# Expert choice of a block kernel: one-hot rows written by tensor_scalar, index lookup by comparing candidate rows

## Chip, cores and metric

The kernel runs on one core of a Trainium2 chip. The metric is the device time of one execution in microseconds (us), lower is better. PE is TensorE, PEld its weight loads, DVE is VectorE, ACT is ScalarE, POOL is GpSimd, SP is SyncE.

## The reference, cut to what matters

Two blocks run one after the other on 256 tokens of width 1024. The change touches the feed-forward part of the first block, a product-key expert retrieval over 16384 experts. For each block of 128 tokens:

```python
q = (t @ w_query).reshape(PEER_BLOCK, PEER_HEADS, 2, PEER_DQ // 2)   # 8 heads, two halves of 128
s1 = einsum('thd,nd->thn', q[:, :, 0], k1)                           # 128 scores per half
s2 = einsum('thd,nd->thn', q[:, :, 1], k2)
v1, i1 = lax.top_k(s1, 16)
v2, i2 = lax.top_k(s2, 16)
cand_s = v1[..., :, None] + v2[..., None, :]                         # 16 x 16 sums
cand_i = i1[..., :, None] * 128 + i2[..., None, :]
top_s, pos = lax.top_k(cand_s.reshape(...), 16)
idx = take_along_axis(cand_i.reshape(...), pos)                      # the 16 experts of a head
g = softmax(top_s)
act = gelu(einsum('thkd,td->thk', expert_u[idx], t))
y = einsum('thk,thkd->td', g * act, expert_v[idx])
```

## The kernel before

No expert row is gathered. The kernel computes gelu(u t) for all 16384 experts, 128 experts at a time (a "key row", 128 of them), multiplies by a dense weight W[token, i1, i2] that is zero where an expert was not chosen, and multiplies by the whole of `expert_v`. W is made of one-hot rows: for each token a 128 x 128 matrix, product of a one-hot over i2 (`O2`) and a weighted one-hot over i1 (`O1`), summed over the 128 choices that lie on the partitions.

The part around the change has four stages.

1. **Query** (`query`, L1065): eight heads of projections, scores, and the top 16 of each half on DVE (`top16`, L1104).
2. **Choice** (`choose`, L1117), for each of two token blocks `t`. Only 50 of the 256 sums can be among the top 16 (`CAND`). DVE adds them (`cs`), POOL adds the 50 matching indices (`ci`, L1135), DVE takes the top 16 of each head. Then 128 instructions at L1160, one for each head and rank, compare a row of 50 positions with the chosen position, multiply by `ci` and sum: that is the index lookup. Its result is split into i1 and i2 (L1165 to L1168), three PE transposes (L1172) put weight, i1 and i2 of all choices on the partitions, and `gT`, `i1T`, `i2T` are written.
3. **One-hots** (`peer_w_steps`, L1184): 64 groups of four tokens. `hot` (L1190) writes with three DVE instructions of fp16 a block `O2` of 128x512, a block `eq` of 128x512 and a block `O1` of 128x1024 (the weight is split in two halves, hence twice the size). The token is the fastest index of these tiles, so PE reads each token's 128 columns with a step of four elements. Eight matmuls (L1212) make one PSUM bank, ACT copies it to `S` (L1214), and every fourth group `S` is sent to the DRAM tensor `Wd` (L1218).
4. **Rows** (loop from L1401): key rows, reading back of W, product with `expert_v`.

Key rows need no choice, only the hidden state. So 38 of them (`RUN`) run ahead of time beside stages 2 and 3 through `run_ahead` (L1357). One such row is 8 PE transposes (L1233), two ACT copies (L1235), two DVE subtractions (`utl`, L1236), 24 matmuls of 256 columns (`peer_a`, L1287) and a gelu on ACT (L1297). Two rows go ahead of the choice, 28 are dealt out over the 21 yields of `choose`, 8 over the first 44 groups of the one-hots. Each engine works its own queue in order, and the program order places the rows between the steps of the other work:

```python
for n, _ in enumerate(self.choose(*top, pick)):
    run_ahead(28 * (n + 1) // 21 - 28 * n // 21)
```

Beside them run `ada` steps (L337: matmuls of modulation weights, 16 calls in each of the two stages) and from group 46 on `group_steps` (L1251), which prepares the hidden state for the later rows. The rows that follow on the 38 wait on DVE for the last one-hot instruction (`lastO`) and on PE for the last one-hot matmul (`lastW`).

Of the kernel before, what the change touches and what calls it, by code (L numbers as in the profile page):

```python
# [29 lines left out]
         "z8:l1a1 v0 z9:l1a2b1 v1 z2:l9b2 g0 z3:b2 g1 xb no w4:o2")  # L30


C_ID, C_MASK, C_EYE, C_IOTA, C_TRI, C_INV, C_ROT, C_N = 0, 128, 448, 480, 608, 736, 737, 865


def const_array():
    c = np.zeros((128, C_N), np.float32)
    p = np.arange(128)
    c[:, C_ID:C_ID + 128] = np.eye(128)
    s = (p % 32)[:, None]  # L40
    t = np.arange(32)[None, :]
    for n, h in enumerate(SMALL):
        same = s // (2 * h) == t // (2 * h)
        c[:, C_MASK + 64 * n:C_MASK + 64 * n + 32] = same & (s // h % 2 == 0) & (t // h % 2 == 1)
        c[:, C_MASK + 64 * n + 32:C_MASK + 64 * n + 64] = same & (s // h % 2 == 1) & (t // h % 2 == 0)
    c[:, C_EYE:C_EYE + 32] = s == t
    c[:, C_IOTA:C_IOTA + 128] = np.arange(128)[None, :]
    c[:, C_TRI:C_TRI + 128] = p[:, None] < p[None, :]
    c[:, C_INV] = 10000.0 ** (-(2 * (p % 32)) / 64)
    rot = np.zeros((128, 128), np.float32)  # L50
    for m in range(128):
        b, r = divmod(m, 64)
        if r < 32:
            rot[b * 64 + r + 32, m] = -1.0
        else:
            rot[b * 64 + r - 32, m] = 1.0
    c[:, C_ROT:C_ROT + 128] = rot
    return c


# [62 lines left out]
class B:  # L123
# [894 lines left out]
        self.modT(self.hh, self.hl, self.xo, m[:, 1, 0:8], m[:, 0, 8:16])  # L1018


    CAND = ((0, 1, 16), (1, 1, 8), (2, 1, 5), (3, 1, 4), (4, 1, 3), (5, 3, 2), (8, 8, 1))
    NCAND = 50

    RUN, GAP = 38, 5
    NGA = RUN + GAP + 1
    TB, WG = 16, 16
# [29 lines left out]
    def peer_keys(self):  # L1056
        nc = self.nc
        self.kr = self.tk.tile([128, 2, 128], F32, name="kr")
        nc.gpsimd.dma_start(out=self.kr, in_=self.I["peer_sub_keys"][0].rearrange("s n d -> n s d"))
        self.kT = self.tk.tile([128, 2, 128], F32, name="kT")  # L1060
        self.iotaT = self.pp.tile([128, 128, 4], F16, name="iotaT")
        nc.gpsimd.iota(self.iotaT, pattern=[[1, 128], [0, 4]], base=0, channel_multiplier=0,
                       allow_small_or_imprecise_dtypes=True)

    def query(self):  # L1065

# [45 lines left out]
    def cand(self, tag):  # L1112

        t = self.tk.tile([128, 2, 256], F32, tag=tag, name=tag, bufs=2).rearrange("p a b -> p (a b)")
        return t[:, :8 * self.NCAND].rearrange("p (h c) -> p h c", h=8)

    def choose(self, vals, idx, res):  # L1117

        nc = self.nc
        pp = self.tk  # L1120
        NC = self.NCAND
        gT = pp.tile([128, 256], F32, name="gT")
        i1T = self.pp.tile([128, 256], F16, name="i1T")
        i2T = self.pp.tile([128, 256], F16, name="i2T")
        for t in range(2):
            fi = pp.tile([128, 2, 8, 16], F32, tag="fi", name="fi")
            nc.vector.tensor_copy(fi, idx[:, t])
            nc.vector.tensor_scalar(fi[:, 0], fi[:, 0], 128.0, None, op0=ALU.mult)
            cs = self.cand("qT")
            ci = self.cand("sc")  # L1130
            for dst, a, b, eng in ((cs, vals[:, t, 0], vals[:, t, 1], nc.vector), (ci, fi[:, 0], fi[:, 1], nc.gpsimd)):
                o = 0
                for a0, na, w in self.CAND:
                    ov = dst[:, :, o:o + na * w].rearrange("p h (a b) -> p h a b", a=na)
                    eng.tensor_tensor(ov, bcast(a[:, :, a0:a0 + na].rearrange("p h (a o) -> p h a o", o=1), (128, 8, na, w)),  # L1135
                                      bcast(b[:, :, 0:w].rearrange("p h (o b) -> p h o b", o=1), (128, 8, na, w)), op=ALU.add)
                    o += na * w
            cs2 = self.cand("sc2")
            tv = pp.tile([128, 8, 16], F32, tag="tv", name="tv", bufs=2)
            ti = pp.tile([128, 8, 16], U32, tag="ti", name="ti", bufs=2)  # L1140
            tf = pp.tile([128, 8, 16], F32, tag="tf", name="tf", bufs=2)
            for h in range(8):
                self.top16(tv[:, h, :], ti[:, h, :], cs[:, h, :], cs2[:, h, :])
            yield

            tw = pp.tile([128, 8, 16], F32, tag="tw", name="tw", bufs=2)
            nc.vector.tensor_tensor(tw, tv, bcast(tv[:, :, 0:1], (128, 8, 16)), op=ALU.subtract)
            tv = tw
            nc.scalar.activation(tv, tv, AF.Exp)
            sm = pp.tile([128, 8], F32, tag="sm", name="sm", bufs=2)  # L1150
            nc.vector.tensor_reduce(sm, tv, axis=AX.X, op=ALU.add)
            nc.vector.reciprocal(sm, sm)
            nc.vector.tensor_tensor(tv, tv, bcast(sm.rearrange("p (h o) -> p h o", o=1), (128, 8, 16)), op=ALU.mult)

            nc.vector.tensor_copy(tf, ti)
            sel = pp.tile([128, 8, 16], F32, tag="sel", name="sel", bufs=2)
            for h in range(8):
                for j in range(16):
                    scr = pp.tile([128, NC], F32, tag="scr", name="scr", bufs=6)
                    nc.vector.scalar_tensor_tensor(scr, self.iota[:, :NC], tf[:, h, j:j + 1], ci[:, h, :], op0=ALU.is_equal,  # L1160
                                                   op1=ALU.mult, accum_out=sel[:, h, j:j + 1])
                yield
            si = pp.tile([128, 2, 128], I32, tag="si", name="si")
            sf = pp.tile([128, 2, 128], F32, tag="sf", name="sf")
            nc.vector.tensor_copy(si[:, 0], sel.rearrange("p h j -> p (h j)"))  # L1165
            nc.vector.tensor_scalar(si[:, 1], si[:, 0], 127, None, op0=ALU.bitwise_and)
            nc.vector.tensor_scalar(si[:, 0], si[:, 0], 7, None, op0=ALU.arith_shift_right)
            nc.vector.tensor_copy(sf, si)  # L1168
            p = self.bank("t")
            ts = slice(128 * t, 128 * t + 128)  # L1170
            for n, a in enumerate((tv.rearrange("p h j -> p (h j)"), sf[:, 0], sf[:, 1])):
                nc.tensor.transpose(p[:, 128 * n:128 * n + 128], a, self.id)  # L1172
            nc.scalar.activation(gT[:, ts], p[:, 0:128], AF.Copy, scale=32768.0)
            nc.vector.tensor_copy(i1T[:, ts], p[:, 128:256])
            nc.vector.tensor_copy(i2T[:, ts], p[:, 256:384])
            yield

        g2 = self.pp.tile([128, 2, 256], F16, name="g2")
        nc.vector.tensor_copy(g2[:, 0], gT)
        nc.vector.tensor_tensor(g2[:, 1], gT, g2[:, 0], op=ALU.subtract)  # L1180
        res.extend((g2, i1T, i2T))
        yield

    def peer_w_steps(self, Wd, g2, i1T, i2T):  # L1184
# [4 lines left out]

        def hot(t4):  # L1190

            ts = slice(4 * t4, 4 * t4 + 4)
            O2 = self.wp.tile([128, 128, 4], F16, tag="O2", name="O2", bufs=2)
            O1 = self.wp.tile([128, 2, 128, 4], F16, tag="O1", name="O1", bufs=2)
            eq = self.wp.tile([128, 128, 4], F16, tag="eq", name="eq")
            bt = (128, 128, 4)
            nc.vector.tensor_tensor(O2, self.iotaT, bcast(i2T[:, ts].rearrange("p (o t) -> p o t", o=1), bt), op=ALU.is_equal)
            nc.vector.tensor_tensor(eq, self.iotaT, bcast(i1T[:, ts].rearrange("p (o t) -> p o t", o=1), bt), op=ALU.is_equal)
            bt = (128, 2, 128, 4)
            self.lastO = nc.vector.tensor_tensor(O1, bcast(eq.rearrange("p (o i) t -> p o i t", o=1), bt),  # L1200
                                    bcast(g2[:, :, ts].rearrange("p i (o t) -> p i o t", o=1), bt), op=ALU.mult)
            return O2, O1
        nxt = hot(0)
        for t4 in range(64):
# [4 lines left out]
            p = self.bank("acc")  # L1209
            for t in range(4):  # L1210
                for n in range(2):
                    self.lastW = nc.tensor.matmul(p[:, 128 * t:128 * t + 128], O2[:, :, t], O1[:, n, :, t], start=(n == 0),  # L1212
                                                  stop=(n == 1))
            nc.scalar.activation(S[:, :, o:o + 4], p.rearrange("p (t i) -> p i t", t=4), AF.Copy)  # L1214
            if t4 < 63:
# [105 lines left out]
    def peer(self, before=None, after=None):  # L1321
# [3 lines left out]
        with ExitStack() as cx:  # L1325
# [51 lines left out]
            with self.pool("topk") as self.tk:  # L1377
# [2 lines left out]
                pick = []  # L1380
                run_ahead(2)
                for n, _ in enumerate(self.choose(*top, pick)):
                    run_ahead(28 * (n + 1) // 21 - 28 * n // 21)
                    if n < 16:
                        self.ada(1)
            with self.pool("W") as self.wp:
                left = self.RUN - len(gas)
                groups = self.group_steps()
                for n, _ in enumerate(self.peer_w_steps(Wd, *pick)):
                    run_ahead(min(left, left * (n + 1) // 44) - min(left, left * n // 44))  # L1390
                    if n >= 46:
                        next(groups, None)
                    if n % 4 == 2:
                        self.ada(1)
# [913 lines left out]
```

## Time and profile before

| | |
|---|---|
| time, median of 3 runs | 2721.43 us (2721.31 to 2723.54) |
| time of the profiled execution | 2725.57 us |
| its span, first to last instruction | 2723.7 us |
| mean granted TensorE clock | 0.967 |
| busy: PE, DVE, ACT, POOL | 94%, 76%, 56%, 12% |

A busy share is the time in which at least one instruction of the engine was running. Matmuls are pipelined, so PE may be busy and not at its peak. On DVE an instruction's duration overlaps the next one's by some 0.08 us when nothing is waited for, so the distance between two starts says what an instruction costs in a stream.

### The profile page before, as it was taken

To read this page: it belongs to the slowest core of one execution; us is meant where nothing else is said; L and a number is where in the kernel's file an instruction comes from. 1 tells how busy PE (TensorE), PEld (TensorE's weight loads), DVE (VectorE), ACT (ScalarE), POOL (GpSimd) and SP (SyncE) were. 2 spreads that over 40 slices of the span, in tenths; PEclk is the share of its full clock that TensorE was granted. 3 is DMA by queue.
4 is the path that set the end of the run, shared out by engine and by line. 5 is a ranking of instruction groups with operands and counts; after the bars stand their busy time and mean duration, and the time that the engine had idled before them with its cause. 6 is when DMAs were issued, how large, how long until landed. Compare 5 with 4: busy or idle time off the path is not lost. (4 is left out here: it accounts for less than half of the span.)

```text
span 2723.7 us, 44417 instructions
## 1 busy us (share of the span) xinstructions
PE 2570.4 (94%) x17241; PEld 2183.4 (80%) x17241; DVE 2067.3 (76%) x3610; ACT 1523.6 (56%) x2172; POOL 335.5 (12%) x405
## 2 busy tenths in 40 slices
PE   6999799998999999999788999989999999999997
PEld 4888698976888888877688999878787877877875
DVE  4658789878766666646676555769999999999997
ACT  2344344444544444445564444757777777777775
POOL 2545100000111111122120000100101001011010
PEclk8998899997999999999899999989999999999999
DMA  7553345487889889875534554359999999999993
GB/s 272 179 186 95 109 169 205 145 283 249 230 255 262 255 248 269 263 282 182 165 112 140 186 186 139 116 180 338 338 358 334 346 342 340 355 336 334 353 332 133
DMA packets 314316, 653.75 MB, mean 240 GB/s; under 512 B 14226, under 2 KB 148264, under 8 KB 302832
## 3 DMA queue, kind: packets, MB, share of 16 engines
q1 hardware_dynamic: 303632, 582.50, 64.4%
q10 hardware_dynamic: 9392, 67.51, 6.6%
q8 instruction: 137, 2.24, 0.3%
q0 software_dynamic: 1072, 0.82, 0.1%
q14 instruction: 83, 0.68, 0.1%
HBM read 632.95 MB, written 17.83 MB: 239 GB/s over the span
## 5 line engine op out<-in xcount | busy, mean ns | idle before, releaser
L290 DVE TENSOR_TENSOR wlo<-ring,whi 128x1024 fp32r<-128x1024 f32 x785 | 967.1, 1252 | 231.5 <-ACT whi L286 226.4
L286 ACT ACTIVATE whi<-ring 128x1024 fp32r<-128x1024 f32 x785 | 821.4, 1056 | 440.0 <-PE acc L398 99.7
L397 PE MATMUL acc<-wlo,xh 128*128 128x512 f32 x768 | 307.7, 401 | 1.3 <-DVE wlo L290 1.2
L398 PE MATMUL acc<-whi,xl 128*128 128x512 f32 x768 | 304.1, 396 | 0.0
L396 PE MATMUL acc<-whi,xh 128*128 128x512 f32 x768 | 301.6, 400 | 0.0
L398 PE MATMUL w<-hh,utl 128*128 128x256 f32 x1024 | 292.8, 286 | 0.2 <-DVE utl L1248 0.2
L396 PE MATMUL w<-hh,uth 128*128 128x256 f32 x1024 | 291.6, 285 | 0.0
L397 PE MATMUL w<-hl,uth 128*128 128x256 f32 x1024 | 286.8, 281 | 0.0
L396 PEld LDWEIGHTS w<-hh,uth 128*128 128x128 f32 x1024 | 193.3, 189 | 28.9 <-ACT gh L1308 20.1
L397 PE MATMUL acc<-wlo,gh 128*128 128x512 f32 x512 | 204.5, 400 | 1.6 <-DVE wlo L290 1.6
L398 PE MATMUL acc<-whi,gl 128*128 128x512 f32 x512 | 200.6, 393 | 0.0
L398 PEld LDWEIGHTS w<-hh,utl 128*128 128x128 f32 x1024 | 193.1, 189 | 3.3 <-issue 1.7
L397 PEld LDWEIGHTS w<-hl,uth 128*128 128x128 f32 x1024 | 192.8, 188 | 2.5
L1309 POOL TENSOR_TENSOR gl<-g,gh 128x256 fp32r<-128x256 f32 x128 | 99.0, 774 | 776.8 <-ACT gh L1308 393.8
L1247 ACT ACTIVATE uth<-ut 128x512 fp32r<-128x512 f32 x180 | 104.5, 624 | 156.1 <-issue 76.4
L396 PE MATMUL acc<-whi,gh 128*128 128x512 f32 x512 | 180.9, 397 | 3.4 <-ACT gh L1308 3.4
L1248 DVE TENSOR_TENSOR utl<-ut,uth 128x512 fp32r<-128x512 f32 x180 | 118.7, 697 | 81.1 <-ACT uth L1247 81.0
L397 PEld LDWEIGHTS acc<-wlo,xh 128*128 128x128 f32 x768 | 144.7, 188 | 39.9 <-DVE wlo L290 4.5
L396 PEld LDWEIGHTS acc<-whi,xh 128*128 128x128 f32 x768 | 144.7, 188 | 34.7 <-ACT xh L2144 0.3
L398 PEld LDWEIGHTS acc<-whi,xl 128*128 128x128 f32 x768 | 144.7, 188 | 32.9 <-DVE xl L2145 0.6
L397 PE MATMUL w<-wlo,mh 128*128 128x512 f32 x384 | 156.3, 407 | 5.6 <-DVE wlo L290 5.5
L2202 POOL TENSOR_TENSOR x<-x,moeroom 128x512 f32<-128x512 f32 x30 | 54.7, 1843 | 845.4 <-DVE moeroom L2201 845.4
(590 smaller groups left out, 5872.4 us busy)
## 6 DMA issues: line engine op xcount, KB each, us to landing
ring<-in_moe_w_gate_dram SPq DMA_DIRECT2D x79, 1024.0 KB, 6.2
ring<-in_moe_w_up_dram SPq DMA_DIRECT2D x79, 1024.0 KB, 5.8
ring<-in_moe_w_down_dram SPq DMA_DIRECT2D x78, 1024.0 KB, 6.2
ring<-in_peer_v_dram SPq DMA_DIRECT2D x64, 1024.0 KB, 8.5
ada<-in_ada_w_dram ACTq DMA_DIRECT2D x48, 1024.0 KB, 6.5
ring<-in_peer_u_dram SPq DMA_DIRECT2D x180, 256.0 KB, 5.8
ring<-in_w_in_dram SPq DMA_DIRECT2D x36, 1024.0 KB, 5.6
ring<-in_peer_u_dram SPq DMA_DIRECT2D x19, 1024.0 KB, 5.0
```

What stands on the lines that cost most here:

```text
L286: nc.scalar.activation(hv, src, AF.Copy)
L290: (eng or nc.vector).tensor_tensor(lv, src, hv, op=ALU.subtract)
L396: mm(o, ah, bh, start=start, stop=False)
L397: mm(o, ah, bl, start=False, stop=False)
L398: return mm(o, al, bh, start=False, stop=stop)
L1247: nc.scalar.activation(uh[:, b4], ut, AF.Copy)
L1248: nc.vector.tensor_tensor(ul[:, b4], ut, uh[:, b4], op=ALU.subtract)
L1309: nc.gpsimd.tensor_tensor(gl, g, gh, op=ALU.subtract)
L2202: (nc.vector if last and i > 1 else nc.gpsimd).tensor_tensor(self.x[:, t, c], self.x[:, t, c], tmp, op=ALU.add)
```

## The change

The lookup no longer scans 50 positions for each choice. The 50 candidates are 16 runs, one for each rank of the first half; `BEGIN` holds where each run starts. A choice at position `pos` belongs to the last run that begins at or before it, so its i1 is the sum of the differences of the sorted i1 list over all runs with begin <= pos, and its i2 is found in the same way from `pos` minus the run's begin. Comparisons, products and folding sums run in fp16 on four heads at once (128 x 1024 elements and less); ACT spreads the differences (`dx`). The POOL index sums and the split into i1 and i2 are gone.

The one-hots are laid out with the 128 columns of a token together, and each is written by its own `tensor_scalar`, with the token's i1, i2 and weight as per-partition scalars: 12 instructions of 128 elements for a group, where three of 512, 512 and 1024 stood. The scalars are kept in fp32. `choose` yields 19 times, and 18 rows (2 and 16) go beside the choice, 20 over the first 56 groups; `group_steps` starts at group 56.

```diff
@@ peer_keys
-        self.iotaT = self.pp.tile([128, 128, 4], F16, name="iotaT")
-        nc.gpsimd.iota(self.iotaT, pattern=[[1, 128], [0, 4]], base=0, channel_multiplier=0, ...)
+        self.rows16 = self.tk.tile([128, 3, 16, 16], F16, name="rows16")
+        for n, c in enumerate((C_IOTA, C_BEG, C_BEG + 16)):
+            nc.gpsimd.tensor_copy(self.rows16[:, n], bcast(self.K[:, c:c + 16].rearrange("p (a o) -> p a o", o=1), (128, 16, 16)))
+        self.iota16 = self.pp.tile([128, 128], F16, name="iota16")
+        nc.gpsimd.tensor_copy(self.iota16, self.iota)
@@ choose
             fi = pp.tile([128, 2, 8, 16], F32, tag="fi", name="fi")
+            df = pp.tile([128, 2, 8, 16], F32, tag="df", name="df")
             nc.vector.tensor_copy(fi, idx[:, t])
-            nc.vector.tensor_scalar(fi[:, 0], fi[:, 0], 128.0, None, op0=ALU.mult)
+            nc.vector.tensor_copy(df[:, :, :, 0:1], fi[:, :, :, 0:1])
+            for s in range(2):
+                nc.vector.tensor_tensor(df[:, s, :, 1:16], fi[:, s, :, 1:16], fi[:, s, :, 0:15], op=ALU.subtract)
...
-            for h in range(8):
-                for j in range(16):
-                    scr = pp.tile([128, NC], F32, tag="scr", name="scr", bufs=6)
-                    nc.vector.scalar_tensor_tensor(scr, self.iota[:, :NC], tf[:, h, j:j + 1], ci[:, h, :], op0=ALU.is_equal,
-                                                   op1=ALU.mult, accum_out=sel[:, h, j:j + 1])
+            def total(P, dst):
+                n = 16
+                while n > 2:
+                    n //= 2
+                    nc.vector.tensor_tensor(P[:, :, 0:n], P[:, :, 0:n], P[:, :, n:2 * n], op=ALU.add)
+                for d, i in dst:
+                    nc.vector.tensor_tensor(d, P[:, i:i + 4, 0], P[:, i:i + 4, 1], op=ALU.add)
+            for h0 in (0, 4):
...
+                    nc.scalar.activation(dx[s], bcast(df[:, s, hs].rearrange("p h (a o) -> p h a o", o=1), sh), AF.Copy)
...
+                nc.vector.tensor_tensor(ge, row(1), at(pos[:, hs]), op=ALU.is_le)
+                nc.vector.tensor_tensor(P[:, 0:4], ge, dx[0], op=ALU.mult)
+                nc.vector.tensor_tensor(P[:, 4:8], ge, row(2), op=ALU.mult)
+                total(P, ((sv[:, 0, hs], 0), (beg, 4)))
                 yield
+                nc.vector.tensor_tensor(beg, pos[:, hs], beg, op=ALU.subtract)
+                nc.vector.tensor_tensor(ge, row(0), at(beg), op=ALU.is_le)
+                nc.vector.tensor_tensor(P[:, 0:4], ge, dx[1], op=ALU.mult)
+                total(P[:, 0:4], ((sv[:, 1, hs], 0),))
+                yield
@@ hot
-            nc.vector.tensor_tensor(O2, self.iotaT, bcast(i2T[:, ts].rearrange("p (o t) -> p o t", o=1), bt), op=ALU.is_equal)
-            nc.vector.tensor_tensor(eq, self.iotaT, bcast(i1T[:, ts].rearrange("p (o t) -> p o t", o=1), bt), op=ALU.is_equal)
-            self.lastO = nc.vector.tensor_tensor(O1, bcast(eq...), bcast(g2[:, :, ts]...), op=ALU.mult)
+            O2 = self.wp.tile([128, 4, 128], F16, tag="O2", name="O2", bufs=3)
+            O1 = self.wp.tile([128, 4, 2, 128], F16, tag="O1", name="O1", bufs=2)
+            for t in range(4):
+                i = slice(4 * t4 + t, 4 * t4 + t + 1)
+                nc.vector.tensor_scalar(O2[:, t], self.iota16, i2T[:, i], None, op0=ALU.is_equal)
+                for n in range(2):
+                    self.lastO = nc.vector.tensor_scalar(O1[:, t, n], self.iota16, i1T[:, i], g2[:, n, i], op0=ALU.is_equal,
+                                                         op1=ALU.mult)
@@ matmul of the one-hots
-                    self.lastW = nc.tensor.matmul(..., O2[:, :, t], O1[:, n, :, t], ...)
+                    self.lastW = nc.tensor.matmul(..., O2[:, t], O1[:, t, n], ...)
@@ peer
-                    run_ahead(28 * (n + 1) // 21 - 28 * n // 21)
+                    run_ahead(16 * (n + 1) // 19 - 16 * n // 19)
...
-                    run_ahead(min(left, left * (n + 1) // 44) - min(left, left * n // 44))
-                    if n >= 46:
+                    run_ahead(min(left, left * (n + 1) // 56) - min(left, left * n // 56))
+                    if n >= 56:
                         next(groups, None)
```

## Rows read from the trace of the kernel before

**Rows 1.** Busy time of each engine by stage; PEclk is the granted TensorE clock.

```profile
405.00:518.00 113.00, 106.38 (x888) 98.81 (x889) 104.50 (x763) 47.85 (x87) 3.72 (x14) 1.00 0.52 180
518.00:590.00 72.00, 72.00 (x652) 64.16 (x651) 52.33 (x105) 31.21 (x62) 0.00 (x0) 1.00 0.74 235
590.00:649.00 59.00, 47.52 (x347) 33.78 (x349) 55.98 (x119) 28.64 (x52) 0.00 (x0) 0.63 0.58 227
...
700.00:1300.00 600.00, 598.44 (x3591) 498.29 (x3591) 396.01 (x608) 280.00 (x485) 94.67 (x125) 1.00 0.82 248
```

**Rows 2.** Groups of instructions by shape, 405 to 518 us (busy us, mean ns).

```profile
L1160 DVE SCALAR_TENSOR_TENSOR scr<-K,tf,sc 128x50 f32<-128x50 f32 x256 | 52.3, 263 | 0.0
...
L1236 DVE TENSOR_TENSOR utl<-t,uth 128x512 fp32r<-128x512 f32 x52 | 35.5, 682 | 7.1 <-ACT uth L1235 6.8
...
L1160 DVE DVE_READ_ACCUMULATOR scr<-K,tf,sc 128x1 f32 x256 | 20.3, 79 | 0.0
```

**Rows 3.** Timeline of ACT at the end of the choice (start us, duration us).

```profile
483.57 0.38 ACT L1297 ACTIVATE ga<-w 128x256 f32<-128x256 f32 x1 [0.60 <-PE w L398]
...
513.05 0.38 ACT L1297 ACTIVATE ga<-w 128x256 f32<-128x256 f32 x1 [0.59 <-PE w L398]
...
517.35 0.28 ACT L1173 ACTIVATE gT<-t 128x128 f32<-128x128 f32 x1 [0.18 <-PE t L1172]
```

**Rows 4.** Timeline of DVE in the lookup.

```profile
466.25 0.69 DVE L1236 TENSOR_TENSOR utl<-t,uth 128x512 fp32r<-128x512 f32 x1
466.86 0.26 DVE L1160 SCALAR_TENSOR_TENSOR scr<-K,tf,sc 128x50 f32<-128x50 f32 x1
...
467.04 0.27 DVE L1160 SCALAR_TENSOR_TENSOR scr<-K,tf,sc 128x50 f32<-128x50 f32 x1
...
468.77 0.08 DVE L1160 DVE_READ_ACCUMULATOR scr<-K,tf,sc 128x1 f32 x1
```

**Rows 5.** Groups of instructions by shape, 518 to 649 us.

```profile
L1212 PE MATMUL acc<-O,O 128*128 128x128 f16 x512 | 70.9, 296 | 11.2 <-DVE O L1200 11.1
...
L1200 DVE TENSOR_TENSOR O<-eq,g 128x1024 f16<-128x1024 f16 x64 | 44.0, 688 | 1.2
...
L1197 DVE TENSOR_TENSOR O<-iotaT,i2T 128x512 f16<-128x512 f16 x64 | 27.0, 421 | 17.1 <-PE acc L1212 16.9
...
L337 PE MATMUL acc<-ada,cs 128*32 128x512 f32 x64 | 10.6, 673 | 0.3 <-DMA ada<-in_ada_w_dram 0.3
```

**Rows 6.** Timeline of DVE late in the one-hots.

```profile
612.73 0.42 DVE L1197 TENSOR_TENSOR O<-iotaT,i2T 128x512 f16<-128x512 f16 x1
...
614.13 0.42 DVE L1197 TENSOR_TENSOR O<-iotaT,i2T 128x512 f16<-128x512 f16 x1
```

**Rows 7.** Timeline of the weight loads of one group, early in the one-hots.

```profile
522.76 0.82 PEld L1212 LDWEIGHTS <-O 128*128 128x128 f16 x8
```

**Rows 8.** Single lines on DVE: duration in ns, min/median/max, first and last start.

```profile
L1197 DVE TENSOR_TENSOR O<-iotaT,i2T x64: 415/423/429, 518.8 to 646.2; 128x512 f16<-128x512 f16 x64
...
L1128 DVE TENSOR_SCALAR fi<-fi x2: 201/210/219, 415.0 to 423.5; 128x128 f32<-128x128 f32 x2
...
L2153 DVE TENSOR_SCALAR C<-K,place x16: 272/274/288, 1816.5 to 2519.4; 128x128 f32<-128x128 f32 x16
...
L1452 DVE TENSOR_SCALAR Wr<-Wr x1: 281/281/281, 1260.2 to 1260.2; 128x256 f32<-128x256 f32 x1
...
L1474 DVE TENSOR_SCALAR mbias<-Wr x2: 341/342/342, 1261.1 to 1261.7; 128x256 f32<-128x256 f32 x2
...
L240 DVE TENSOR_SCALAR xn<-x,mv x2: 752/752/753, 1324.9 to 1326.3; 128x1024 f32<-128x1024 f32 x2
...
L1015 DVE TENSOR_SCALAR xo<-x,mv x2: 812/812/812, 335.1 to 336.8; 128x1024 f32<-128x1024 f32 x2
```

**Rows 9.** Timeline of DVE where L2153 runs twice in a row.

```profile
1816.47 0.47 DVE L2153 TENSOR_SCALAR C<-K,place 128x128 f32<-128x128 f32 x2
1816.86 0.16 DVE L2025 TENSOR_SCALAR w<-w 128x2 f32<-128x2 f32 x1
```

## What is predicted

> **What bounds the kernel now.** I read the stages first (busy time by stretch), then the groups of the two stages that change, then the timelines of ACT, DVE and PE inside them, and at last single lines for the price of an operation that the two stages do not hold. In the choice, 405 to 518 us, two engines are nearly full: PE 106.4 and DVE 104.5 of 113 us [rows 1]. PE is the one that sets the end: the gelus of the rows come every (513.05 - 483.57) / 8 = 3.685 us, without a DVE wait between them, and the last choice values leave PE only at 517.35, behind the last of these rows [rows 3]. A row beside the choice therefore costs 3.69 us of time. The one-hot stage has two halves. [...] There a group takes 614.13 - 612.73 = 1.40 us, one DVE group after the other [rows 6], while PE needs 0.82 us for its weight loads of a group [rows 7]. After 700 us PE is busy for 598.4 of 600 us [rows 1], so a shift of the one-hots' end goes through to the end of the kernel.
>
> **How I price a DVE instruction.** In a stream, starts lie closer than durations say: the subtraction `utl` lasts 0.68 to 0.69 us but its successor starts after 466.86 - 466.25 = 0.61 [rows 2, 4]. So I take 0.08 us off each duration where nothing waits. Fp16 tensor_tensor: 421 ns at 512 elements, 688 at 1024 [rows 5], that is 0.152 us plus 0.52 ns an element; fp32 at 512 elements lasts 682 [rows 2], by the same fixed part 1.04 ns an element.
>
> **The choice.** Removed from DVE: 256 lookups, of which one starts every (468.77 - 467.04) / 9 = 0.192 us [rows 4]: 49.2 us. With the split of the index and the multiplication by 128 (four instructions of the 0.2 us kind of L1128 [rows 8] and a cast for each token block), about 51 us. The POOL sums fall away too; POOL is busy for 3.7 us of 113 and nothing gets faster by it [rows 1]. Added: one half block of four heads has six fp16 tensor_tensor of 1024 elements (6 x 0.688), two of 512, two of 256, one of 128 and four of 64. By the line above: 4.13 + 0.84 + 0.57 + 0.22 + 0.74 = 6.5 us, each at full duration because each reads what the one before wrote. Four half blocks make 26 us, the differences `df` 1.5 more. Should the comparison or the broadcast rows run at fp32's rate, a half block has about 10.5 us and the lookup some 43; nothing can bring it far below 26. ACT gets eight copies of 1024 elements. The nearest row is its gelu, 0.38 us for 256 elements [rows 3], so about 1 to 1.5 us each, 12 at most; it is busy for 47.9 of 113 us [rows 1] and loses the copies of 11 rows, so that is hidden. POOL's four small copies stand where its iota stood, on an idle engine, long before the first lookup. The 32 further constants cost nothing that is waited for, and the 16 `ada` calls stay in this stage.
>
> Rows: ahead of the last transposes stood 2 + 28 x 19 // 21 = 27 rows, now 2 + 16 x 17 // 19 = 16. Eleven rows less make 11 x 3.685 = 40.5 us less of PE. DVE: 104.5 - 51 + 27.5 - 11 x 2 x 0.61 = 67.6 us, against 113.8 - 40.5 = 73 us of PE. So PE still sets the end, by little, and the lookup is now a chain of dependent instructions in a queue that also holds `utl`. I add 4 us for that. The choice ends 36.5 us earlier; with the slow lookup (43) DVE would need 84 us and the gain is 28.
>
> **The one-hots.** No row shows tensor_scalar on fp16, so it is bounded. With immediates alone, 128 fp32 elements last 210 ns and 256 last 281 [rows 8]: 0.55 ns an element, half of what fp32 tensor_tensor needs. A per-partition scalar costs on top, each time: 274 against 210 ns (one pointer, L2153 against L1128), 342 against 281 (one, L1474 against L1452), 812 against 752 (two against one, L1015 against L240) [rows 8]. That is 0.060 to 0.064 us for each pointer, and it is not hidden in a stream: two L2153 in a row take 1816.86 - 1816.47 = 0.39, 0.195 each [rows 9]. The new `O2` instruction has one pointer, the two `O1` instructions two each. Lower bound: the elements cost nothing, 0.195 less 0.071 for 128 elements is 0.124 us, with a second pointer 0.186; a group then has 4 x (0.124 + 2 x 0.186) = 2.0 us. Upper bound: as fp32, 0.195 and 0.257, 2.84 us a group. I take half of fp32's time for the elements, since fp16 halves it in tensor_tensor (0.52 against 1.04 ns): 0.160 and 0.222, 2.42 us a group. Even the lower bound is above the 1.40 us of before. The 64 groups need 64 x 2.42 = 155 us of DVE.
>
> [...]
>
> The other DVE work of the stage: 42 `utl` for the 22 rows that now lie behind the choice (21 rows, one having its transposes ahead), 42 x 0.61 = 25.6, and about 5.5 for `group_steps` and the rest. The same count for before, 64 x 1.40 + 20 x 0.61 + 5.5 = 107.3, meets the 52.3 + 56.0 of [rows 1]. So DVE has 155 + 31 = 186 us. PE has 64 x 0.82 + 22 x 3.69 + 10.6 for `ada` [rows 5] + some 6 = 150. DVE becomes the bound of the whole stage. `O1` has two buffers, a row holds PE for 3.7 us in one piece, and the second `utl` of a row waits for matmuls and ACT behind it, so I allow 5% of stalls: 196 us, against 130 before (518.8, the first `O2` [rows 8], to 649). That is +66. Contiguous reads may shorten PE's 0.82 us; PE is not the bound then and it gains nothing. Three buffers of `O2` and the later `group_steps` cost nothing while DVE is behind.
>
> **The sum.** -36.5 + 66 = +29.5 us. The profiled execution took 2725.6 us, its span 2723.7, the median 2721.4; the sum holds for either, on the median 2751.
>
> **The rivals.**
> *The clock falls beside the rows.* With PE busy at 150 of 196 us it lies between the half that kept 1.00 and the half that had 0.63 [rows 1]. [...]
> *Fp16 is no faster than fp32 in tensor_scalar.* 2.84 us a group, 182 + 31 = 213 us, 224 with stalls: -36.5 + 94, 2779.
> *The other side: the scalars are fetched beside the instruction before.* Then an instruction costs L1128's 0.210 less 0.08 of overlap, less half of 0.071 for fp16, 0.095, and twelve 1.1 us a group [rows 8], DVE 73 + 31 = 104 us; PE's 150 are the bound again, 154 with stalls: -36.5 + 24 = -12.5, 2709. It decides when a group stays under about 2.0 us (166 us of stage, less 5%, less 31, over 64), a mean of 0.165 us an instruction against my 0.20. [...] Rows 9 speaks against it, with instructions of the same shape one behind the other.
> *The rows do not move as written.* 27 rows stood ahead of the last transposes before, as the program order has it, so I give this nothing.
>
> **How the numbers follow.** The forecast 0.56, the clock 0.13, fp32's rate 0.11, hidden scalars 0.12, a group near 2.0 us (change within 0.2%, about what a measurement of this kernel can tell from none) 0.08. Faster 0.12, same 0.08, slower 0.80. Taken alone, the forecast spans 2738 to 2764: the choice's gain from 28 to 41, stalls from 2 to 8%. The range reaches from 2730, which leaves out the hidden scalars and most of the near break-even, to 2785, the fp32 rate with its stalls.
>
> **What would show it.** Right: the first one-hot at 478 to 488 us; tensor_scalar starts 0.16 and 0.22 us apart; DVE at 93% or more and PE with waits on the one-hots between 485 and 675; PE again full behind it. Wrong: starts 0.10 us apart, or PE full and DVE waiting on `acc` in that stretch; in the choice, a DVE that works past PE's rows.

## The result and the profile after

The changed kernel takes 2741.23 us (median of 5; 2740.32 to 2742.78) against 2723.54 for the kernel before: ratio 1.0064, 95% interval 1.0053 to 1.0075. That is 17.7 us slower; the spans of the profiled executions differ by 17.3 (2741.0 against 2723.7). The direction and the mechanism are those of the forecast, the size is 12 us below it.

By stage (same columns as [rows 1]):

```profile
405.00:476.00 71.00, 68.30 (x571) 61.37 (x570) 65.78 (x285) 38.37 (x65) 0.00 (x0) 1.00 0.60 209
476.00:619.00 143.00, 131.00 (x1152) 106.58 (x1151) 139.95 (x608) 58.66 (x112) 0.00 (x0) 0.98 0.64 221
619.00:663.00 44.00, 33.44 (x154) 16.07 (x157) 44.00 (x207) 15.93 (x30) 0.00 (x0) 0.51 0.23 96
720.00:1320.00 600.00, 598.45 (x3594) 498.02 (x3593) 396.96 (x607) 281.39 (x487) 95.10 (x126) 1.00 0.80 247
```

The choice is short, and PE is fuller in it than it was (68.3 of 71 us, [rows 1] had 106.4 of 113). Then DVE is the full engine through the whole one-hot stage, 140.0 of 143 us and 44.0 of 44; PE has gaps, and from 619 to 663 us its mean granted clock is 0.51. From 720 us on it is [rows 1] again, with PE full.

The end of the choice on ACT, with the gelus of the last two rows (start, duration; to be held against [rows 3]):

```profile
469.81 0.39 ACT L1327 ACTIVATE ga<-w 128x256 f32<-128x256 f32 x1 [0.57 <-PE w L404]
...
473.29 0.38 ACT L1327 ACTIVATE ga<-w 128x256 f32<-128x256 f32 x1 [0.58 <-PE w L404]
473.57 0.27 ACT L1203 ACTIVATE gT<-t 128x128 f32<-128x128 f32 x1
```

The last choice values come at 473.6 instead of 517.35, again right behind a row. The groups of the one-hot stage, 476 to 663 us, which answer to [rows 5]:

```profile
L1230 DVE TENSOR_SCALAR O<-iota,i1T,g 128x128 f16<-128x128 f16 x512 | 125.6, 303 | 3.0 <-PE acc L1242 3.0
L1242 PE MATMUL acc<-O,O 128*128 128x128 f16 x512 | 80.1, 236 | 12.4 <-DVE O L1230 9.7
L1228 DVE TENSOR_SCALAR O<-iota,i2T 128x128 f16<-128x128 f16 x256 | 52.9, 243 | 0.1
```

and two groups late in it on DVE, which answer to [rows 6]:

```profile
642.89 0.57 DVE L1228 TENSOR_SCALAR O<-iota,i2T 128x128 f16<-128x128 f16 x3
643.38 1.42 DVE L1230 TENSOR_SCALAR O<-iota,i1T,g 128x128 f16<-128x128 f16 x6
644.71 0.24 DVE L1228 TENSOR_SCALAR O<-iota,i2T 128x128 f16<-128x128 f16 x1
...
645.32 0.57 DVE L1228 TENSOR_SCALAR O<-iota,i2T 128x128 f16<-128x128 f16 x3
```

A group repeats after 645.32 - 642.89 = 2.43 us, where one late in the stage before took 1.40 [rows 6]. Three instructions of `O2` fill 643.38 - 642.89 = 0.49, 0.163 each; with the duration's overlap of 0.08 us taken off, `O1` costs 0.303 - 0.08 = 0.223. Six `O1` in a row fill 644.71 - 643.38 = 1.33, 0.222 each, the same. DVE waits only 3.0 us for PE, while PE idles 12.4 us ahead of one-hot matmuls, 9.7 of them for `O1`. The prediction left open whether contiguous reads shorten PE's part. The weight loads of a group where nothing holds them, at a granted clock of 1.00 (to be held against [rows 7]):

```profile
510.11 0.45 PEld L1242 LDWEIGHTS <-O 128*128 128x128 f16 x8
```

Eight loads follow each other in 0.45 us and not 0.82, and their matmuls, from the first start to the last end, in 0.62 and not 1.11: read with its columns together, a one-hot matmul costs PE about half at this clock.

### The profile page after: what moved, and what is told of

Read it like the earlier page. It is cut to its first block, busy times and chain, and to the rows that moved or that the text cites. A ratio compares the mean times of both kernels' runs of the same rounds, so it can differ in the third digit from the quotient of the medians.

```text
span 2741.0 us, 44537 instructions
## 1 busy us (share of the span) xinstructions
PE 2579.3 (94%) x17241; PEld 2171.1 (79%) x17241; DVE 2108.2 (77%) x3731; ACT 1530.1 (56%) x2180; POOL 332.2 (12%) x394
```

## The experiments

Times are medians, ratios those to the kernel before on the same chip. "Hot" is the start of the first one-hot instruction, "stage" the time from there to the last one-hot matmul: 518.8 and 130.0 before, 475.9 and 186.9 after.

**Lookup and rows without the new one-hots.** From the changed kernel:

```diff
-    nc.vector.tensor_scalar(O2[:, t], self.iota16, i2T[:, i], None, op0=ALU.is_equal)      # and O1
+    nc.vector.tensor_tensor(O2, self.iotaT, bcast(i2T[:, ts]...), op=ALU.is_equal)         # eq, O1: hot() of before
```

> The new lookup with the one-hots of before (interleaved, three tensor_tensor a group) and the new dealing of rows, 18 and 20. My theory, the twelve scalar instructions of a group cost 2.43 us where 1.40 stood and that is the loss: the choice still ends some 43 us earlier than before, a group is 1.40 us again, PE (150 us of work) becomes the bound of the one-hot stage, which takes 150 to 155 us against 130; -43 + 22 = -21 us against the kernel before. Rival, the rows moved beside the one-hots are the loss: the one-hot stage stays near 187 us and the time near +17.

2708.74 us, ratio 0.9949 (0.9936 to 0.9963): 13.8 us faster than before where 21 were expected, and 32 faster than the changed kernel. Hot is at 474.7, the stage takes 156. Busy time in the two stages:

```profile
405.00:474.70 69.70, 66.98 (x560) 60.06 (x558) 64.61 (x280) 37.29 (x63) 0.00 (x0) 1.00 0.59 210
474.70:630.70 156.00, 150.82 (x1310) 136.17 (x1312) 121.19 (x242) 75.00 (x141) 0.00 (x0) 0.96 0.67 230
```

PE is the bound of both, 150.8 of 156 us in the second with the 150 us of work that the prediction had counted, and DVE has room. So the 20 rows beside the one-hots are not the loss; the way of writing the one-hots is.

**New one-hots alone**, in the kernel before (`hot`, its index tiles and the matmul's operands of the change, nothing else):

> The new one-hots with the lookup of before and its rows, 28 and 8. My theory: the choice ends as before (518 us), the one-hot stage needs 64 x 2.43 + 20 x 0.61 + 6 = 174 us of DVE against 130, so +44 us against the kernel before. Rival, the rows are the loss: about 0.

2778.69 us, ratio 1.0209 (1.0193 to 1.0224), +56 where +44 was expected; stage 183.8. DVE was busy for the 174 us that were counted (174.6 of 185). The remainder shows in the waits of the stage (waiter, what it waited for: us, times, longest):

```profile
DVE O L1199 <- PE acc L1211: 9.7, 7, 3.9
PEld acc L337 <- DMA ada<-in_ada_w_dram: 9.1, 5, 3.6
```

DVE waited 9.7 us for PE to free `O1`, and PE's weight loads stood 9.1 us in front of modulation weights that were still on their way. I had not counted that. Whether the second wait is the cause of the first was not tested.

**New lookup alone**, rows dealt as before:

```diff
-    run_ahead(16 * (n + 1) // 19 - 16 * n // 19)       # 20 rows over 56 groups, group_steps from 56
+    run_ahead(28 * (n + 1) // 19 - 28 * n // 19)       # 8 rows over 44 groups, group_steps from 46; hot() of before
```

> The new lookup alone: one-hots of before and rows dealt as before, 28 and 8. My theory, PE with its rows sets the end of the choice and DVE's saving there is worth nothing until rows move: the choice ends at 515 to 519 us as before, the one-hot stage stays at 130, within 4 us of before. Rival, DVE's lookups set the choice's end: the choice 20 us shorter, -20 us.

2715.94 us, ratio 0.9967 (0.9954 to 0.9980): 7.0 us faster, more than I allowed. Hot is at 512.1, the stage unchanged at 130.5. **Rows alone**, the kernel before with 16 and 20:

> The kernel before with only the rows dealt out anew, 16 over the choice and 20 over the first 56 groups. My theory, PE's work is the same and DVE's 91 us of the choice set its end: the choice 15 to 20 us shorter, the one-hots (PE 150 us of work) 20 to 25 longer, together +2 to +8 us against before. Rival, the rows are the loss: +17. Rival, the gap of the clock late in the one-hots is what matters and rows there fill it: -10 or better.

2726.41 us, ratio 1.0016 (1.0007 to 1.0025): +3.9, as expected. The choice in both, the lookup alone first:

```profile
405.00:512.00 107.00, 105.67 (x903) 99.00 (x896) 80.84 (x311) 55.56 (x96) 0.00 (x0) 1.00 0.55 193
```
```profile
405.00:503.00 98.00, 82.28 (x663) 71.73 (x662) 95.91 (x752) 37.11 (x67) 3.73 (x14) 1.00 0.49 168
```

With the lookup alone PE is full (105.7 of 107) and DVE has 26 us to spare; with the rows alone DVE is full (95.9 of 98). Alone they bring the one-hots' start forward by 6.7 and 15.7 us, together (the first experiment) by 44: each takes away the bound that the other leaves.

**The scalars one by one.** `O1` with a constant for its weight, then with two constants, `O2` with an fp16 scalar in the second:

```diff
-    nc.vector.tensor_scalar(O1[:, t, n], self.iota16, i1T[:, i], g2[:, n, i], op0=ALU.is_equal, op1=ALU.mult)
+    nc.vector.tensor_scalar(O1[:, t, n], self.iota16, i1T[:, i], 1.0 - n, op0=ALU.is_equal, op1=ALU.mult)            # one scalar
+    nc.vector.tensor_scalar(O1[:, t, n], self.iota16, 5.0, 2048.0 * (1 - n), op0=ALU.is_equal, op1=ALU.mult)         # none
```

> The changed kernel with a constant (1 or 0) in place of the weight in the tensor_scalar of O1, so that it has one per-partition scalar instead of two; the weights of the experts are left out of the result. My theory, each per-partition scalar costs 0.06 us: starts of O1 lie 0.16 us apart, a group has 12 x 0.163 = 1.96 us, the one-hot stage 156 to 160 us instead of 187, the kernel about 28 us faster than the changed one, near -11 us against before. Rival, the number of instructions is the price and not their scalars: no change, +17.

> The changed kernel with two constants in O1 (index 5, weight of even size) and an fp16 scalar in O2 in place of fp32; choice of the first index and weight are left out of the result. My theory, the per-partition scalars are the price: O1 starts 0.10 us apart instead of 0.22, a group 4 x (0.16 + 0.20) = 1.45 us, PE becomes the bound, the one-hot stage some 135 to 145 us instead of 187. An fp16 scalar costs as much as an fp32 one: O2 stays at 0.16. Rival, the instruction count: O1 stays above 0.16 and the stage above 165.

With other expert weights the second block gets other data, and both kernels took near 4000 us; in the first the time up to 2200 us has nearly the busy times of the kernel before, so what is longer lies later, and I read only the stage of either (the second ran once). The line of `O1` with one scalar, then with none, and a stretch of DVE of the latter:

```profile
L1230 DVE TENSOR_SCALAR O<-iota,i1T x512: 241/246/257, 475.6 to 643.7; 128x128 f16<-128x128 f16 x171
```
```profile
L1230 DVE TENSOR_SCALAR O<-iota x512: 178/184/197, 478.7 to 611.6; 128x128 f16<-128x128 f16 x171
...
603.18 0.90 DVE L1230 TENSOR_SCALAR O<-iota 128x128 f16<-128x128 f16 x8
603.99 0.41 DVE L1228 TENSOR_SCALAR O<-iota,i2T 128x128 f16<-128x128 f16 x2
```

184, 246 and 303 ns for none, one and two scalars: about 0.06 us each. Eight without scalars fill 603.99 - 603.18 = 0.81, 0.10 each. The stage fell from 186.9 to 168.8 and to 133.6. So it is the scalars and not the count of twelve: without the two of `O1`, twelve instructions make 4 x (0.163 + 2 x 0.10) = 1.45 us a group, about the 1.40 of the three before. The first stage was expected at 156 to 160; DVE's busy time there is 155.2 as counted, but it waited 9.3 us for PE. In the second PE became the bound, as expected: busy for 131.2 of 133.6 us, DVE for 124.1. The fp16 scalar of `O2` costs as much as the fp32 one (245 ns median; the changed kernel, fp32, has 244).

**Which side sets PE's pace.** In the trace a one-hot matmul is a weight load on PEld and a MATMUL on PE (512 of each at L1242). Of the two operands in the call, `O2` is called the weights here and `O1` the moving side. Three ways to write the one-hots on top of the new lookup and rows:

```diff
+    O2 by four tensor_scalar, contiguous; eq and O1 by tensor_tensor, step 4          # e7
+    O1 by eight tensor_scalar, contiguous; O2 by tensor_tensor, step 4                # e8
+    O2 [128, 2, 128, 2], O1 [128, 2, 2, 128, 2]: two tokens interleaved, step 2       # e9
+    nc.vector.tensor_tensor(O2, two, bcast(i2T[:, ts].rearrange("p (a o t) -> p a o t", a=2, o=1), bt), op=ALU.is_equal)
+    nc.vector.tensor_tensor(eq, two, bcast(i1T[:, ts].rearrange("p (a o t) -> p a o t", a=2, o=1), bt), op=ALU.is_equal)
+    for a in range(2):
+        self.lastO = nc.vector.tensor_tensor(O1[:, a], bcast(eq[:, a:a + 1], bt), bcast(g2[:, :, i]...), op=ALU.mult)
```

> New lookup and rows 18 and 20; O2 (the weights) contiguous by four tensor_scalar with one scalar each, eq and O1 (the moving side) interleaved by tensor_tensor as before. DVE 4 x 0.163 + 0.45 + 0.61 = 1.71 us a group, 140 us in all. If the stride of the weights sets PE's pace, the matmuls come 0.056 us apart, PE's work falls to 127 us and the one-hot stage takes 142 to 148 us: -25 to -30 us against before. If the stride of the moving side sets it, they stay 0.118 apart, PE's 150 us are the bound and the time is that of the lookup-only kernel, -14 to -18.

> New lookup and rows 18 and 20; O1 (the moving side) contiguous by eight tensor_scalar with two scalars each, O2 (the weights) interleaved by one tensor_tensor. DVE 8 x 0.223 + 0.34 = 2.12 us a group, 167 us in all, so the one-hot stage some 168 to 172 us and the time near before's, -2 to +2. If the moving side alone sets PE's pace, matmuls on a full clock come 0.056 us apart; if both sides must be contiguous, 0.118.

> New lookup and rows 18 and 20; one-hots by four tensor_tensor a group and no scalars, interleaved by two tokens instead of four, so that PE reads with a step of two elements (4 bytes). DVE 0.34 + 0.45 + 2 x 0.34 = 1.48 us a group, 126 us in all. If PE's pace goes with the step, matmuls come under 0.09 us apart, PE's work falls below 135 us and the one-hot stage to 135 to 142 us: -30 to -35 us against before, ahead of the lookup-only kernel. If any step above one costs the same, 0.118 apart, the stage 156 as there, -14.

The eight matmuls of a group at a clock of 1.00, from the first start to the last end, in this order:

```profile
522.80 1.09 PE L1247 MATMUL acc<-O,O 128*128 128x128 f16 x8
```
```profile
487.87 0.64 PE L1247 MATMUL acc<-O,O 128*128 128x128 f16 x8
```
```profile
523.90 0.63 PE L1245 MATMUL acc<-O,O 128*128 128x128 f16 x8
```

Contiguous weights change next to nothing (1.09 us; weights and moving side interleaved by four had 1.11 in the kernel before, at 522.76). A contiguous moving side brings 0.64 although the weights have a step of four, and a step of two on both sides is as good (0.63; the changed kernel, all contiguous, has 0.62 at 510.11). The times: e7 2717.12 us, ratio 0.9978 (0.9969 to 0.9987), 6 us faster than before and not the 14 to 18 expected. Its stage took 166 us, and the bound changes sides in it: PE was full up to 611 us (busy for 133.3 of 134.8), then, with the rows used up, DVE was (30.1 of 31.2, a group every 1.71 us, the price expected). The expectation had PE full to the end. e8 2721.13, ratio 0.9990 (0.9980 to 0.9999), 2.4 us faster, at the edge of what was expected; stage 168.0. e9 2688.61, ratio 0.9871 (0.9854 to 0.9887): 35 us faster than before, 53 faster than the change. Its two stages:

```profile
405.00:476.90 71.90, 69.27 (x579) 62.09 (x575) 66.89 (x291) 39.60 (x66) 0.00 (x0) 1.00 0.58 206
476.90:614.40 137.50, 129.28 (x1310) 112.59 (x1312) 122.94 (x306) 74.08 (x141) 0.00 (x0) 0.96 0.76 260
```

PE has 129 us of work in the second where the lookup-only kernel had 151, and DVE 123. This version beats both kernels.

## Why the prediction was right, and where its sizes were off

**The price of the scalars held.** Forecast 0.160 and 0.222 us, measured 0.163 and 0.223; a group 2.42 against 2.43. The rows that priced it lay in quite other parts of the kernel [rows 8, 9]. DVE's work in the stage was put at 186 us and its busy time is 184. The bound moved from PE to DVE, as said. Without scalars the trace shows starts 0.10 us apart, with one and two 0.163 and 0.223.

**The stalls were over-sized.** I allowed 5%, 10 us, for `O1`'s two buffers and the rows on PE. DVE waited 3.0 us; the stage is 187 us and not 196, +57 and not +66.

**The choice was under-sized.** -36.5 forecast, -42.9 measured, 6.4 more. Two parts of that step were wrong. I took all of the choice's time before as PE's work, but PE was idle for 6.6 us of it [rows 1], 4.3 behind `utl` in DVE's queue and 2.3 behind modulation weights still on their way (waiter, what it waited for: us, times, longest):

```profile
PE t L1233 <- DVE utl L1236: 4.3, 5, 1.1
PE acc L337 <- DMA ada<-in_ada_w_dram: 2.3, 2, 1.2
```

With the lookup alone PE is idle for 1.3 us, and hot comes 6.7 earlier (512.1); in the changed kernel it is idle for 2.7, which is 3.9 less than before. And the 4 us added for a chain of dependent instructions did not appear. The other way go 1.5 us: PE's work was 68.2 us where 107.2 - 40.5 = 66.7 were counted, and by their gelus 17 rows, not 16, ran ahead of the last choice values. So 4 + 3.9 - 1.5 = 6.4. The lookups, priced at 26 us, cost what was said (six of 1024 elements at 0.68 to 0.69 us in a half block),

```profile
L1188 DVE TENSOR_TENSOR ge<-rows,pos 128x1024 f16<-128x1024 f16 x4 | 2.7, 679 | 0.0
...
L1189 DVE TENSOR_TENSOR P<-ge,sc 128x1024 f16<-128x1024 f16 x4 | 2.7, 687 | 0.1
```

and DVE sat idle for 5.2 of 71 us. The broadcast rows and the comparison run at fp16's rate (679 and 687 ns, where [rows 5] have 688 for 1024 elements). That a link costs its full duration was right where nothing stands between it and the next: `L1196` reads what `L1195` wrote right before it and starts 437.30 - 436.57 = 0.73 us behind, while `L1195` lasts 0.69; the 0.08 of overlap is gone.

**Behind the stage** 3.3 us were lost that the sum did not have: the last one-hot matmul is 14.0 us later than before, the end 17.3. The first product with W follows it by 22.0 us where it was 20.6. The 30 us behind the stage, before and after:

```profile
648.80:678.80 30.00, 26.34 (x182) 22.30 (x182) 22.92 (x36) 14.33 (x28) 3.18 (x3) 0.92 1.01 322
662.80:692.80 30.00, 25.65 (x160) 21.10 (x160) 22.10 (x35) 13.10 (x25) 2.13 (x2) 0.81 1.01 320
```

The granted clock is lower there, (0.92 - 0.81) x 30 = 3.3 us of full clock. That is the size of the loss; that it is its cause was not tested. So 29.5 - 6.4 - 9.1 + 3.3 = 17.3, the difference of the spans.

**The rivals.** Scalars fetched beside the instruction before: excluded by 0.10, 0.163 and 0.223 us for none, one and two. Fp32's rate: excluded by 0.163. The clock: it did fall, to 0.51 from 619 to 663 us, but DVE is full there and PE busy for 33 of 44 us, so within the stage it cost nothing that these rows show; beside the rows, from 476 to 619 us, it stayed at 0.98. What a key row costs at a lower clock was not measured. That PE gains nothing from contiguous reads held only because DVE was the bound: they halve its one-hot matmuls (one every 0.056 us and not every 0.116), and that was the larger prize (e9 is 35 us faster than before, the first experiment without it 13.8), which the change bought with scalars and could not use.

## What to carry to other kernels

Before many small tensor_scalar take the place of a few broadcast tensor_tensor, count the per-partition scalars as well as the instructions: here 20 scalars a group at 0.06 us are 1.2 us of its 2.43, more than the 1.03 by which the group grew. An operand layout can serve both engines: two tokens interleaved kept DVE's wide instructions and gave PE nearly the pace of contiguous reads (a matmul every 0.059 us against 0.056). Work that moves between stages and work that gets cheaper should be tried together, since each may only uncover the bound that the other removes.

## What the runs showed that was not expected

The step of the moving operand set the pace of these matmuls of 128 fp16 columns. From the groups above, less one matmul's duration, over seven: with a step of four elements (8 bytes) one starts every (1.11 - 0.30) / 7 = 0.116 us at a clock of 1.00 (one lasts 0.30 [rows 5]), with two elements (4 bytes) every (0.63 - 0.22) / 7 = 0.059, contiguous every (0.62 - 0.23) / 7 = 0.056 (one lasts 0.22 and 0.23); the step of the weights did not matter (1.09 us a group with contiguous weights, 1.11 with a step of four). Two groups of the kernel before, the first at a granted clock of 1.00, the second at 0.50, and one with a step of two (e9) at 0.50:

```profile
522.76 1.11 PE L1212 MATMUL acc<-O,O 128*128 128x128 f16 x8
```
```profile
642.19 1.11 PE L1212 MATMUL acc<-O,O 128*128 128x128 f16 x8 [0.29 <-DVE O L1200]
```
```profile
607.47 1.03 PE L1245 MATMUL acc<-O,O 128*128 128x128 f16 x8 [0.21 <-DVE O L1233]
```

At 0.50 the step of four costs what it costs at 1.00, 0.116 us, while the step of two goes from 0.059 to (1.03 - 0.31) / 7 = 0.103 (one lasts 0.31). So the step of two gains 0.057 us a matmul at a clock of 1.00 and 0.013 at 0.50.
